# A roll of an 8192 x 8192 matrix, copied from HBM to HBM: 16 long DMAs that step by 64 rows, or 128 DMAs of 64 neighbouring rows

## The chip, the cores and the metric

One core of a Trainium2 chip. The metric is the time of one execution in microseconds on the device; where several executions are timed, their median is quoted. All ratios below are the mean time of one kernel's fast runs over the mean of the kernel before's fast runs of the same rounds, on the same chip, so they are not quite the ratio of the medians beside them.

## The reference

```python
def setup_inputs():
    return {"x": np.random.randn(8192, 8192).astype(np.float32), "shift": 100}

def reference(x, shift):
    return np.roll(x, shift, axis=1)
```

A row is 32 KiB. Each row moves right by 100 floats (400 B), and its last 100 floats come round to the front. No arithmetic is done; 268 MB have to be read and 268 MB written.

## The kernel before

With `s = 100`, `a = 128` (the shift rounded up to 512 B) and `g = 28`, the bulk of each row, 8,064 floats, is copied by DMA straight from `x` to `out`, from two issuing engines in turn (SP and ACT). In the DRAM view `j e c w`, `e` is outermost inside a DMA, so DMA engine `e` gets rows `64 c + 4 e + j` for one `j` and 32 values of `c`: its successive packets are 64 rows, or 2 MiB, apart.

```python
    engines = [nc.sync, nc.scalar]
    # ... cut
    xm = x.rearrange("(c e j) w -> j e c w", e=16, j=4)
    om = out.rearrange("(c e j) w -> j e c w", e=16, j=4)
    depth = n_rows // 64 // 4
    for c in range(4):
        for j in range(4):
            if a < n_cols:
                cs = slice(c * depth, (c + 1) * depth)
                engines[j % 2].dma_start(out=om[j, :, cs, a:], in_=xm[j, :, cs, g:n_cols - s])
```

The first 128 columns of the output go through SBUF: GpSimd issues the loads and stores, VectorE puts the pieces together. The change doesn't touch this part.

```python
    for k in range(n_st):                       # 2 steps of 4096 rows
        # ... tiles t and h cut
        for q in range(1, Q):
            nc.gpsimd.dma_start(out=t[:, q - 1], in_=lead)      # 3 loads, 512 B runs
        nc.gpsimd.dma_start(out=h[:, Q - 1, :, :s], in_=xt[k, Q - 1, :, :, n_cols - s:])
        nc.vector.tensor_copy(h[:, :Q - 1, :, :s], t[:, :, :, :s])
        if g > 0:
            nc.gpsimd.dma_start(out=h[:, 0, :, s:], in_=xt[k, 0, :, :, :g])
            nc.vector.tensor_copy(h[:, 1:, :, s:], t[:, :, :, s:])
        tiles.append(h)
    for k, h in enumerate(tiles):
        for q in range(Q):
            nc.gpsimd.dma_start(out=ot[k, q, :, :, :a], in_=h[:, q])
```

## Time and profile before

| | kernel before |
|---|---|
| median of 3 runs (first session) | 828.8 us (828.28 to 829.5) |
| span of the profiled execution | 815.4 us |
| row packets, each 32,256 B | 8,192, 4,096 a queue |

The profiled execution was 1.4% shorter than the timed ones.

The lines that carry the bound are in the prediction.

### The profile page before, as it was taken

How to read it: one execution, taken by the hardware profiler on the slowest of the kernel's cores; microseconds unless marked ns; L12 is line 12 of the kernel's file. 1: busy time of each engine (PE TensorE's matmuls, PEld its weight loads, DVE VectorE, ACT ScalarE, POOL GpSimd, SP SyncE). 2: the span in 40 equal slices, each digit the busy share in tenths (PEclk: the TensorE clock that was granted, in tenths of full speed). 3: DMA queues.
4: the chain of work that ended last, by engine and by line, in shares of the span. 5: the costliest groups of instructions: out<-in, count | busy, mean ns of one | idle time of the engine just before them, and what ended most of it. 6: DMA issues, size and time to landing. Idle time of an engine off the chain costs nothing. (4 is left out here: it accounts for less than half of the span.)

```text
span 815.4 us, 93 instructions
## 1 busy us (share of the span) xinstructions
DVE 3.7 (0%) x4; POOL 16.1 (2%) x22
## 2 busy tenths in 40 slices
DVE  0000000000000000000000000000000000000000
POOL 3000001000010000000000000000000000000000
DMA  9999999999999999999999999999999999999996
GB/s 310 341 328 347 330 349 335 337 340 346 338 337 346 338 348 348 347 333 345 340 344 337 349 326 335 334 329 334 335 329 331 329 335 334 332 331 332 329 334 250
DMA packets 10784, 272.63 MB, mean 334 GB/s; under 512 B 544, under 2 KB 544, under 8 KB 2592
## 3 DMA queue, kind: packets, MB, share of 16 engines
q10 hardware_dynamic: 4224, 132.12, 47.0%
q1 hardware_dynamic: 4224, 132.12, 46.9%
q0 software_dynamic: 2336, 8.39, 4.5%
HBM read 268.44 MB, written 268.44 MB: 658 GB/s over the span
## 5 line engine op out<-in xcount | busy, mean ns | idle before, releaser
L76 POOL DMA_DIRECT2D out_dram<-h x8 | 6.9, 954 | 170.1 <-DMA h<-in_x_dram 144.1
L67 POOL DMA_DIRECT2D t<-in_x_dram x6 | 5.4, 910 | 0.8 <-PEq L107 0.8
L69 DVE COPY h<-t 128x2400 f32<-128x2400 f32 x2 | 2.8, 1410 | 208.5 <-DMA t<-in_x_dram 208.5
L71 POOL DMA_DIRECT2D h<-in_x_dram x2 | 1.8, 883 | 28.6 <-DMA t<-in_x_dram 28.6
L68 POOL DMA_DIRECT2D h<-in_x_dram x2 | 1.8, 882 | 27.0 <-DMA t<-in_x_dram 27.0
L72 DVE COPY h<-t 128x672 f32<-128x672 f32 x2 | 1.0, 503 | 0.0
L93 POOL MEMSET const-float32-0.0<- 128x1 f32 x1 | 0.1, 99 | 0.2 <-issue 0.2
L93 POOL MEMSET const-bfloat16-1.0<- 128x1 bf16 x1 | 0.1, 103 | 0.0
L93 POOL MEMSET const-float32-1.0<- 128x1 f32 x1 | 0.1, 99 | 0.0
L93 POOL MEMSET const-uint8-127<- 128x1 uint8 x1 | 0.1, 99 | 0.0
## 6 DMA issues: line engine op xcount, KB each, us to landing
out_dram<-in_x_dram SPq DMA_DIRECT2D x8, 16128.0 KB, 401.3
out_dram<-in_x_dram ACTq DMA_DIRECT2D x8, 16128.0 KB, 400.5
out_dram<-h POOLq DMA_DIRECT2D x8, 512.0 KB, 182.5
t<-in_x_dram POOLq DMA_DIRECT2D x6, 512.0 KB, 118.2
h<-in_x_dram POOLq DMA_DIRECT2D x2, 400.0 KB, 151.3
h<-in_x_dram POOLq DMA_DIRECT2D x2, 112.0 KB, 146.1
```

The source lines that it names most:

```text
L67: nc.gpsimd.dma_start(out=t[:, q - 1], in_=lead)
L68: nc.gpsimd.dma_start(out=h[:, Q - 1, :, :s], in_=xt[k, Q - 1, :, :, n_cols - s:])
L69: nc.vector.tensor_copy(h[:, :Q - 1, :, :s], t[:, :, :, :s])
L71: nc.gpsimd.dma_start(out=h[:, 0, :, s:], in_=xt[k, 0, :, :, :g])
L72: nc.vector.tensor_copy(h[:, 1:, :, s:], t[:, :, :, s:])
L76: nc.gpsimd.dma_start(out=ot[k, q, :, :, :a], in_=h[:, q])
L93: nc = _bacc.Bacc("TRN2", target_bir_lowering=False, num_devices=1)
```

## The change

The intent: each block of 64 neighbouring rows becomes one DMA, with four neighbouring rows for each of the 16 DMA engines. Each engine gets the same rows in all, but in sequence, and there are 128 DMAs in place of 16.

```diff
-    xm = x.rearrange("(c e j) w -> j e c w", e=16, j=4)
-    om = out.rearrange("(c e j) w -> j e c w", e=16, j=4)
-    depth = n_rows // 64 // 4
-    for c in range(4):
-        for j in range(4):
-            if a < n_cols:
-                cs = slice(c * depth, (c + 1) * depth)
-                engines[j % 2].dma_start(out=om[j, :, cs, a:], in_=xm[j, :, cs, g:n_cols - s])
+    for c in range(n_rows // 64):
+        r = slice(64 * c, 64 * (c + 1))
+        if a < n_cols:
+            engines[c % 2].dma_start(out=out[r, a:], in_=x[r, g:n_cols - s])
```

## The prediction

> **What bounds the kernel now.** I read the engine table and the strip of 40 slices first, to see whether any compute engine matters at all.
>
> ```profile
> DVE 3.7 (0%) x4; POOL 16.1 (2%) x22
> DMA  9999999999999999999999999999999999999996
> GB/s 310 341 328 347 330 349 335 337 340 346 338 337 346 338 348 348 347 333 345 340 344 337 349 326 335 334 329 334 335 329 331 329 335 334 332 331 332 329 334 250
> DMA packets 10784, 272.63 MB, mean 334 GB/s; under 512 B 544, under 2 KB 544, under 8 KB 2592
> ```
>
> VectorE and GpSimd together work for 20 us out of 815. The DMA strip is at 9 or more in 39 slices and the rate is flat between 326 and 349 GB/s from the second slice on; only the last slice falls, to 250. So this is a copy that runs at one rate from start to end, and the question is what sets that rate. Next the queues and the issues.
>
> ```profile
> q10 hardware_dynamic: 4224, 132.12, 47.0%
> q1 hardware_dynamic: 4224, 132.12, 46.9%
> q0 software_dynamic: 2336, 8.39, 4.5%
> HBM read 268.44 MB, written 268.44 MB: 658 GB/s over the span
> out_dram<-in_x_dram SPq DMA_DIRECT2D x8, 16128.0 KB, 401.3
> out_dram<-in_x_dram ACTq DMA_DIRECT2D x8, 16128.0 KB, 400.5
> ```
>
> The three queues keep the 16 DMA engines busy for 98.4% of the span (47.0 + 46.9 + 4.5). Each hardware queue has 4,224 packets: 4,096 rows of 32,256 B and 8 DMAs x 16 engines = 128 completion writes. One row packet therefore takes about 0.47 x 16 x 815.4 / 4,096 = 1.50 us. "Always busy" could mean that each engine is at its own limit, or that all of them wait on a shared one. The trace's packet records (my tabulation) separate the two: the shortest row packets take 1.19 us and some 23% of them lie within 50 ns of that; the median is 1.47 us and the 90th percentile 1.83 us. An engine with nothing in its way needs 1.19 us, so 512 rows each would be 512 x 1.19 = 611 us. The other quarter of the row time is waiting for something shared.
>
> Then a table of stretches, chosen so that the GpSimd packets (which the packet records show between about 8 and 464 us of the span) are in the second and not in the third, and engines finish in the fourth and fifth.
>
> ```profile
> 20.00:120.00 100.00, 1.83 (x2) 1.77 (x2) 1.00 1.00 337
> 120.00:440.00 320.00, 1.83 (x2) 6.93 (x8) 1.00 1.00 342
> 480.00:740.00 260.00, 0.00 (x0) 0.00 (x0) 1.00 1.00 332
> 760.00:795.00 35.00, 0.00 (x0) 0.00 (x0) 1.00 0.94 335
> 795.00:815.00 20.00, 0.00 (x0) 0.00 (x0) 1.00 0.63 255
> ```
>
> The last two columns are the DMA share and GB/s. Between 760 and 795 us only 94% of the engines' time is busy, and the rate is no lower (335 against 332): when one engine stops, the others take its share. That is a shared ceiling. And it is one of HBM: a row copy loads HBM twice (read and write), a GpSimd packet once. GpSimd moves 8.39 MB in about 456 us, 18.4 GB/s. Up to 440 us: 2 x (342 - 18.4) + 18.4 = 666 GB/s of HBM traffic; after 480 us: 2 x 332 = 664. The payload rate changes by 3%, the HBM rate by 0.3%. So the kernel's time is 536.9 MB over about 665 GB/s = 807 us, and some 8 us of start and tail. Last, who waits for whom:
>
> ```profile
> SPq L37 <- DMA out_dram<-in_x_dram: 47.6, 4, 16.7
> ```
>
> Only four waits stand before an issue: a queue has four DMAs in flight, its fifth waits for the first to land.
>
> **What the Trainium skill says.** "HBM Reference", section Specifications (TRN2), gives about 716 GB/s for a pair's stack; 665 is 93% of it, so the trace agrees with a ceiling there and leaves at most 7% to win even with perfect HBM behaviour. "DMA: Bandwidth & Descriptors", section Why a DMA increments its semaphore by 16 and not by 1, says that the slowest dimension is divided over the largest k up to 16 that fits: 16 x 32 rows before and 64 rows after both give 16 engines, and the 128 completion writes per queue agree. The same page, section Latency and other measured facts, reports copies losing rate at row pitches of large powers of two: 207 GB/s at 512 KiB, 164 at 2 MiB. The kernel before steps by exactly 64 rows x 32 KiB = 2 MiB from packet to packet of a queue, which is why this change is worth doubting; yet it moves 332 GB/s each way, so its trace does not show that loss. The same page, section Issuing engines are not separate DMA queues, says that DMAs of SP and ACT interleave on the same 16 engines; the nearly equal shares of q1 and q10 agree.
>
> **The change, part by part.** Bytes, row packets (8,192 of 32,256 B) and the rows of each engine (four of every 64) stay. GpSimd's and VectorE's instructions stay, in the same order. What changes:
>
> Issues: 16 DMAs become 128, 64 a queue. The cheapest issue in the trace took 0.61 us on SP and 0.67 on ACT. 64 x 0.65 = 42 us of a sequencer that has 815: hidden.
>
> Completion writes: 256 become 2,048, so 112 more on each engine. The packet records give 9 ns each, and the other queue's next row starts about 10 ns after one. 112 x 9 ns = 1.0 us of an engine's time. As HBM, not the engine, is the ceiling, I count 0 to 1 us, say 0.5.
>
> Depth: still four DMAs in flight a queue (the built program waits on the same four semaphores in turn), but each now has 4 rows per engine for 32. A block of 64 rows takes about 812 / 128 = 6.3 us, a queue gets through one in 12.7 us, and four cover 51 us. When the oldest lands, three others (38 us of work) are queued, against an estimated 2 to 3 us for seeing it and issuing the next. No engine at the common pace runs dry. The median from issue to landing should fall from 401 to about 45 to 51 us.
>
> Skew: no engine may now be more than four blocks (about 51 us) ahead of the slowest. The completion writes show 15 engines within about 10 us of each other, and one that gains after 410 us: 17 us ahead at 501, 27 at 590, 40 at 678, done at 758 us of the span with the others at 797 to 815. The new limit would hold that one a little near the end; by the fourth row of the table above, what it doesn't use the others take. Worth 0 to -2 us in the tail.
>
> Order of rows: an engine's successive packets alternate between two neighbouring blocks 2 MiB apart and then step by 32 KiB, where before they alternated between neighbouring rows 32 KiB apart and then stepped by 2 MiB. At any moment the 16 engines still read and write rows at 128 KiB from each other, which is the larger pattern that HBM sees. I see nothing in the trace that lets me price this term: I set 0, with a spread of about 2%.
>
> Sum: 828.8 + 0.5 - 1 + 0 = about 828 us.
>
> **The rivals.** First, that the 2 MiB step cost HBM efficiency and short steps give it back. For: the skill's pitch measurement. Against: 93% of the stack's figure already. If the ceiling rose by 3% to 685 GB/s, the time would be about 828.8 - 807 x 0.029 = 805 us; I hold more than that to be very unlikely. Second, that it goes the other way: both queues now stand on the same row of two blocks at exactly 2 MiB, and all engines are held within a narrow band of blocks, so addresses that differ only in high bits collide more often. For: the same measurement. Against: HBM traffic stayed at 664 to 666 GB/s whether the engines were 2.5 us apart (first landings) or 10 and more (later), and whichever of the four rows was in turn, so the ceiling seems blind to such patterns. With 3% less it would be 854 us. Third, that the short queue starves: a fast engine waits, or issue latency shows after each landing. If each round of four blocks (16 a queue) lost 2 us it would be +32 us, 861 us; but three blocks are queued behind the oldest, so I give it little. Fourth, that the time is that of the HBM traffic and nothing moves: the base case.
>
> **Range and chances.** The base case gives 826 to 830. The order term has no price from the trace, so the range takes about 1.5% below and 2% above: 815 to 846. Faster by over 2% (below 812) needs more than 678 GB/s: 0.10. Slower by over 2% (above 845) needs a loss in HBM order or starving: 0.13. Within 2%: 0.77.
>
> **What would show it right or wrong.** Right: 5,120 packets on each hardware queue (4,096 + 1,024); DMA strip still 9 throughout; 664 to 668 GB/s of HBM traffic in the steady stretches; median landing near 50 us; about 60 waits before issues on SP, of about 12 us each, with no engine idle behind them. The starving rival would show a DMA share of 0.95 or less in the middle with row packets nearer 1.19 us. The order rivals would show a share of 1.00 with the rate, and the mean of a row packet (1.49 us), changed together. What would make me wrong is an effect of address order on HBM that neither skew nor row index brought out in the kernel before.

## More of the kernel before

```profile
out_dram<-h POOLq DMA_DIRECT2D x8, 512.0 KB, 182.5
t<-in_x_dram POOLq DMA_DIRECT2D x6, 512.0 KB, 118.2
```

A GpSimd DMA is 32 times smaller than one of SP's (512 against 16,128 KB) and still takes 118 to 182 us.

## The result, and the profile after

In the first comparison the changed kernel took 830.78 us (830.12 to 832.05, 6 runs) against 828.66 us (828.28 to 829.5, 6 runs): ratio 1.0026, 95% interval 1.0013 to 1.0039. Two repeats on other chips gave 0.9996 (0.9974 to 1.0017) and 1.0024 (1.0009 to 1.0040). So it is the same within 2%, and probably 0.2% slower.

The page after, first the DMA strip and the queues (packets, MB, share of the engines' time):

```profile
DMA  9999999999999999999999999999999999999996
q10 hardware_dynamic: 5120, 132.12, 48.6%
q1 hardware_dynamic: 5120, 132.12, 45.4%
q0 software_dynamic: 2336, 8.39, 4.7%
out_dram<-in_x_dram SPq DMA_DIRECT2D x64, 2016.0 KB, 51.1
out_dram<-h POOLq DMA_DIRECT2D x8, 512.0 KB, 154.3
t<-in_x_dram POOLq DMA_DIRECT2D x6, 512.0 KB, 102.9
```

Each hardware queue has 4,096 rows and 64 x 16 = 1,024 completion writes (one for each engine at the end of a DMA). A row DMA now lands after 51.1 us (401.3 before), and the strip is still 9 throughout. What the prediction did not name is in the last two lines: GpSimd's DMAs land 13 and 15% sooner (15 and 18% in the two controls, on one chip). Next the waits of SP's own queue (us in total, times, longest):

```profile
SPq L33 <- DMA out_dram<-in_x_dram: 748.3, 60, 15.4
```

SP waits 60 times, 12.5 us each, before it issues: the price of a short queue, paid by a sequencer that has nothing else to do. (Before, the sequencer was no freer: there a single issue of a long DMA held it for 84 us in the median, after for 0.5 us.) Last the stretches of the same windows as in the prediction (last two columns: DMA share, GB/s), of the first profile after:

```profile
20.00:120.00 100.00, 1.83 (x2) 4.39 (x5) 1.00 1.00 329
120.00:440.00 320.00, 1.83 (x2) 4.33 (x5) 1.00 1.00 337
480.00:740.00 260.00, 0.00 (x0) 0.00 (x0) 1.00 1.00 329
760.00:795.00 35.00, 0.00 (x0) 0.00 (x0) 1.00 1.00 332
```

The rates lie 1 to 2% below the first trace of before (337, 342, 332), and it is tempting to read that as the price of the new order. But that trace was of an execution of 817 us, where the timed ones took 828 us and more, and this one is of 832 us. Laid beside each other on one chip, in the controls, the two kernels have the same rates within 2 GB/s.

### The profile page after: what moved, and what is told of

It reads as the page before. It is cut to its first block, busy times and chain, and to the rows that moved or that the text cites. A ratio compares the mean times of both kernels' runs of the same rounds, so it can differ in the third digit from the quotient of the medians.

```text
span 830.2 us, 205 instructions
## 1 busy us (share of the span) xinstructions
DVE 3.7 (0%) x4; POOL 16.1 (2%) x22
## 2 busy tenths in 40 slices
DMA packets 12576, 272.64 MB, mean 328 GB/s; under 512 B 2336, under 2 KB 2336, under 8 KB 4384
## 3 DMA queue, kind: packets, MB, share of 16 engines
q10 hardware_dynamic: 5120, 132.12, 48.6%
q1 hardware_dynamic: 5120, 132.12, 45.4%
q0 software_dynamic: 2336, 8.39, 4.7%
## 6 DMA issues: line engine op xcount, KB each, us to landing
out_dram<-in_x_dram SPq DMA_DIRECT2D x64, 2016.0 KB, 51.1
```

## The experiments

Every variant replaces only the loop that copies the long part of the rows; GpSimd's part stays, and all of them gave the right result. The times in the expectations are mostly put against the first session's 828.7 us (those for two_mib_across and far_spread against 818 us), so the ratios are what to compare.

| run | rows of one DMA engine | distance between engines | DMAs | median us (kernel before) | ratio (95%) |
|---|---|---|---|---|---|
| before_again | steps of 2 MiB | 128 KiB | 16 | 819.9 (819.0) | 1.0006 (0.9982 to 1.0031) |
| after_again | 4 in sequence | 128 KiB | 128 | 818.3 (819.0) | 0.9996 (0.9974 to 1.0017) |
| after_third | 4 in sequence | 128 KiB | 128 | 820.5 (818.3) | 1.0024 (1.0009 to 1.0040) |
| short_stepped | steps of 2 MiB | 128 KiB | 128 | 824.1 (819.0) | 1.0073 (1.0049 to 1.0096) |
| long_sequence | 32 in sequence | 1 MiB | 16 | 820.7 (819.0) | 1.0026 (0.9989 to 1.0063) |
| near_engines | steps of 512 KiB | 32 KiB | 128 | 819.8 (818.0) | 1.0021 (0.9996 to 1.0045) |
| near_long | steps of 512 KiB | 32 KiB | 16 | 824.2 (819.0) | 1.0066 (1.0044 to 1.0088) |
| one_row | 1 a DMA | 32 KiB | 512 | 825.4 (818.0) | 1.0093 (1.0071 to 1.0115) |
| fourteen_engines | 5 in sequence, 14 engines | 160 KiB | 118 | 842.9 (818.0) | 1.0299 (1.0262 to 1.0337) |
| two_mib_across | 4 in sequence | 2 MiB | 128 | 1389 (818.3) | see there |
| far_engines | 4 in sequence | 16 MiB | 128 | 2157 (818.0) | see there |
| far_spread | 4 in sequence | 15.6 MiB | 128 | 827.4 (818.3) | 1.0113 (1.0084 to 1.0142) |

### The two controls

The kernels before and after, unchanged.

> The kernel before, unchanged, as a control: its first profile had a span of 815 us while its timed runs took 828.8, and the changed kernel's profile had 830. All theories: time 828.7, ratio 1.000 within 0.2%. If profiled executions of this kernel really run faster than timed ones, the span is 815 again with 664 GB/s of HBM traffic in the steady part (2 x payload); if the first profile was a lucky chip or execution, the span is 826 to 828 and the steady payload rate 328 to 330 GB/s, the same as after the change.

> The changed kernel, unchanged, as a control on the same chip as the other three. Time 830.8, ratio 1.0026 (0.1 to 0.4% above); steady payload 329 GB/s; 5,120 packets on each hardware queue.

Measured: 819.9 and 818.3 us, in profiles with spans of 818.3 and 816.5 us. Here the profiled executions are not faster than the timed ones, so the first profile of before was not typical of the session in which the 828.8 us were timed. The stretch from 480 to 740 us, before and then after (DMA share, GB/s last):

```profile
480.00:740.00 260.00, 0.00 (x0) 0.00 (x0) 1.00 1.00 332
```

```profile
480.00:740.00 260.00, 0.00 (x0) 0.00 (x0) 1.00 1.00 333
```

On this chip the same rate of 332 and 333 GB/s each way, that is 664 and 666 GB/s of HBM traffic, carries both. The change as a whole is worth nothing here in either direction.

### The two halves of the change, one at a time

short_stepped: DMAs as short as after, rows in the order of before.

```diff
+    depth = 4
+    for c in range(n_rows // 64 // depth):
         for j in range(4):
             ...   # as before
```

> Only half of the change: 128 DMAs of four rows per engine as after, but each DMA's rows step on by 64 rows as before (SP has rows 0 and 2 of each four, ACT rows 1 and 3). Theory A (the 0.26% is the price of 1,792 more completion writes, the order is free): 830 to 832, as after, with 5,120 packets a queue. Theory B (order of rows costs HBM efficiency, the size of the DMA is free): 828 to 829.5, as before. Either way GpSimd's packets should finish at about 395 us of the span rather than 464, if each completion write gives GpSimd's queue one more turn.

long_sequence: DMAs as long as before, rows in sequence.

```diff
+    for c in range(16):
+        r = slice(512 * c, 512 * (c + 1))
+        engines[c % 2].dma_start(out=out[r, a:], in_=x[r, g:n_cols - s])
```

> The other half: 16 DMAs of 32 rows per engine as before, but an engine's rows in sequence, 32 KiB from packet to packet (its 32 rows are neighbours, so engines are 1 MiB apart, where both kernels have 128 KiB). Theory A: 828 to 829.5, as before, 4,224 packets a queue. Theory B: 830 to 832, as after, or further from before, as the sequence is longer. GpSimd's packets end at about 464 us as in the kernel before. A large difference (over 2%) would mean that the distance between engines matters, which both theories leave out.

Measured: 1.0073 and 1.0026, the second with runs from 815 to 827 us and so inconclusive (it also sets the engines 1 MiB apart, so it changes more than the order). Theory A (the completion writes) wanted short_stepped to equal after, whose ratio on this chip was 0.9996; it was 0.7% above. Theory B (the order) wanted it to equal before, and failed as well. Taken by way of short_stepped, the change is two steps that cancel: short DMAs in the old order cost 0.7% (819.0 to 824.1 us), and the new order with DMAs of the same length gives 0.7% back (824.1 to 818.3 us). short_stepped was built only once, so that a build by itself makes such a difference is not excluded; three builds of after lay within 0.3% of each other. The traces say where the 0.7% is: in the stretch from 480 to 740 us short_stepped moves 329 GB/s where the controls move 332 and 333, with the same DMA share of 1.00.

```profile
480.00:740.00 260.00, 0.00 (x0) 0.00 (x0) 1.00 1.00 329
```

So the order of rows seems to move the rate by up to 1% (329 against 333 GB/s with DMAs of the same length), and not in a way that either simple theory orders. One expectation came close: GpSimd's packets ended at about 388 us of short_stepped's span (466 in the control of before), where 395 and 464 were expected.

### Is the ceiling shared, or is it the engines' own?

fourteen_engines: the same rows over 14 engines.

```diff
+    xm = x[:8190].rearrange("(c e j) w -> c e j w", e=14, j=5)
+    om = out[:8190].rearrange("(c e j) w -> c e j w", e=14, j=5)
+    for c in range(117):
+        engines[c % 2].dma_start(out=om[c, :, :, a:], in_=xm[c, :, :, g:n_cols - s])
+    nc.sync.dma_start(out=out[8190:, a:], in_=x[8190:, g:n_cols - s])
```

> Is the bound a shared ceiling or the engines themselves? Blocks of 70 rows over 14 engines instead of 64 over 16 (585 rows for each of 14, and two last rows on two engines), everything else as after. Shared HBM ceiling: 826 to 842 us, same within 2%, the mean row packet falling from about 1.50 to 1.31 us and payload staying at 328 to 335 GB/s while the engines at work are 14 (the page's DMA share then shows about 0.88). Engines bound by their own time per packet: 585 / 512 = 1.14 times as long, 930 to 950 us, packets staying at 1.49 us.

Measured 1.0299, where the shared ceiling wanted up to 2% and the engines' own limit 14%. So the run is clearly slower, and outside the range of the shared ceiling by about one per cent. From its page and its stretches:

```profile
DMA  8888888889888888888888888888888888888853
GB/s 294 345 335 332 333 341 336 342 333 344 337 336 351 336 328 342 328 344 311 340 323 337 325 334 317 331 319 336 325 333 327 319 330 327 327 313 339 322 253 132
...
480.00:740.00 260.00, 0.00 (x0) 0.00 (x0) 1.00 0.86 327
```

With 86% of the engines' time the rate is 327 GB/s, against 332 with all of it. In the packet records the mean of a row fell from 1.50 to 1.34 us (1.31 expected), and 63% of the rows took the 1.19 us that a row needs with nothing in its way (22% in the control). The ceiling is shared among the engines; that it is one of HBM is a further step, taken under one_row. The 3% are in two places: 1.5% in the steady rate, which is 12 us; and a longer tail, where the last two slices (253 and 132 GB/s, 21 us each, against about 330) cost some 18 us, where the one slow slice of before costs 5. Why the steady rate is lower and the tail longer is not shown.

### Do addresses matter at all?

far_engines: engine e has 512 rows of its own, and otherwise everything is as after. near_engines: engines on neighbouring rows.

```diff
 far_engines
+    xm = x.rearrange("(e c j) w -> c e j w", e=16, j=4)
+    om = out.rearrange("(e c j) w -> c e j w", e=16, j=4)
 near_engines
+    xm = x.rearrange("(c j e) w -> c e j w", e=16, j=4)
+    om = out.rearrange("(c j e) w -> c e j w", e=16, j=4)
 both
+    for c in range(n_rows // 64):
+        engines[c % 2].dma_start(out=om[c, :, :, a:], in_=xm[c, :, :, g:n_cols - s])
```

> Does the HBM ceiling depend on addresses at all? As after, but each engine has its own stretch of 512 rows, so that engines stand 16 MiB apart instead of 128 KiB; four rows in sequence, same DMAs and counts. Ceiling blind to order: 829 to 833 us. If far-apart high-power-of-two addresses collide[...]: 10% to 100% slower, 910 us and more, with the DMA share still 1.00 and row packets longer in proportion. In that case the agreement of before and after comes from what they share, the 128 KiB between engines.

> The opposite: as after, but the 16 engines stand on 16 neighbouring rows (32 KiB apart), and an engine steps by 16 rows (512 KiB). Ceiling blind to order: 829 to 833 us. If closeness of the 16 streams matters to HBM, over 1% either way, shown as a row packet mean away from 1.52 us at a DMA share of 1.00.

Measured: near_engines 1.0021; far_engines 2,035 to 2,233 us in four runs, 2.6 times the kernel before by the medians (its runs are too far apart for a ratio; the fastest, which was the one profiled, still took 2.5 times as long). From far_engines' page, and a stretch without GpSimd's packets:

```profile
DMA  9999999999999999999999999999999999999998
GB/s 128 125 139 129 128 135 127 129 135 137 155 132 139 152 132 145 141 144 143 126 129 132 128 144 130 130 140 138 124 133 131 134 129 143 132 128 136 133 130 117
q10 hardware_dynamic: 5120, 132.12, 48.9%
...
1000.00:1500.00 500.00, 0.00 (x0) 0.00 (x0) 1.00 1.00 132
```

The DMA strip looks like that of the kernel before, 9 in every slice, and the rate is 134 in place of 334 GB/s. A row packet takes 3.87 us in the packet records. The same bytes, packets and DMAs in the same number: only the addresses that are in flight together differ. The ceiling is far from blind to them, and the busy strip doesn't show it; only the rate does.

### Which property of the addresses?

two_mib_across: the 2 MiB step that the kernel before takes along one engine is laid across the engines. far_spread: far apart, but 500 rows instead of 512.

```diff
 two_mib_across
+    xm = x.rearrange("(c e k j) w -> c k e j w", e=16, k=16, j=4)     # om alike
+    for c in range(n_rows // 64):
+        engines[c % 2].dma_start(out=om[c // 16, c % 16, :, :, a:],
+                                 in_=xm[c // 16, c % 16, :, :, g:n_cols - s])
 far_spread
+    xm = x[:8000].rearrange("(e c j) w -> c e j w", e=16, j=4)        # om alike
+    for c in range(125):
+        engines[c % 2].dma_start(out=om[c, :, :, a:], in_=xm[c, :, :, g:n_cols - s])
+    ...   # rows 8000 to 8191 as after
```

> The kernel before steps by 2 MiB from packet to packet along one engine. Here the 2 MiB lie across the engines instead: engine e works in block e of sixteen blocks of 64 rows, four rows in sequence, all else as after. If what hurt the run with engines 16 MiB apart is that all engines share the address remainder at 2 MiB (they start each row at the same place in a 2 MiB frame), this is slow too: row packets of 2 to 4 us, 1,100 us and more. If only larger distances hurt[...], this takes 818 to 826 us.

> The engines far apart but with different remainders: engine e has 500 rows of its own (15.6 MiB from engine to engine), and 500 rows are 7 x 64 + 52, so the 16 engines have 16 different remainders at 2 MiB, as in the kernels before and after; the last 192 rows as after. If the shared remainder made the run with 16 MiB slow: back to 818 to 828 us at 330 GB/s. If distance itself did (more of HBM in use at once): again near 2,000 us.

Measured: two_mib_across 1,255 to 1,423 us, 1.7 times by the medians (again no ratio; its runs differ too much, and the profile was of one of the long ones; the fastest took 1.5 times as long). far_spread 1.0113. The steady stretch of both, in this order:

```profile
480.00:740.00 260.00, 0.00 (x0) 0.00 (x0) 1.00 1.00 207
```

```profile
480.00:740.00 260.00, 0.00 (x0) 0.00 (x0) 1.00 1.00 329
```

Engines far apart on different remainders cost about 1%; engines 2 MiB or 16 MiB apart cost a factor. Twelve rows less between engines bring the rate back from 132 to 329 GB/s. The reading I tested, that engines must not share their remainder at 2 MiB (what is left of the address after division by 2 MiB), holds for these two runs, and before, after, near_engines and far_spread all have 16 different remainders. But it isn't the whole rule: in long_sequence engines are 1 MiB apart, which gives only two remainders if they run in step, and it lost 0.3% (0.6% at most, by the interval). Did the deep queue let its engines drift apart? The traces say no. At the start of the span all engines begin their first rows together (within 0.4 us in long_sequence), and the stretch from 5 to 20 us, long_sequence first and then two_mib_across, is

```profile
5.00:20.00 15.00, 0.00 (x0) 3.44 (x4) 1.00 1.00 332
```

```profile
5.00:20.00 15.00, 0.00 (x0) 3.44 (x4) 1.00 1.00 187
```

From 20 to 105 us long_sequence moves 328 GB/s (before_again and after_again 335 and 339), and at the end of that stretch its first DMA lands on all 16 engines within 3.2 us, so they are still in step to about a row. Engines in step on two remainders thus already go at nearly the full rate, and on one remainder they do not. Where between them the loss begins, and why, is left open.

### How short may a DMA be?

one_row: blocks of 16 rows.

```diff
+    for c in range(n_rows // 16):
+        r = slice(16 * c, 16 * (c + 1))
+        engines[c % 2].dma_start(out=out[r, a:], in_=x[r, g:n_cols - s])
```

> Blocks of 16 rows, one row for each engine in a DMA: 512 DMAs, 256 a queue, with four in flight a queue as before. It quarters the queue's depth (about 12.6 us queued) and quadruples the completion writes (8,192 on the two queues). Completion theory, in proportion: after has 112 more for each engine than before and is 2.1 us longer, this has 496 more, so 828.7 + 9.4 = about 838 us. If completion writes are free under the HBM ceiling: 829 to 832. If the short queue starves the engines: over 850 us with a DMA share under 0.95 and row packets nearer 1.19 us. GpSimd's packets, with two turns a row instead of 1.25, end at about 240 to 260 us.

Measured 1.0093, or 7.4 us; the completion theory wanted 9.4, and starving over 21. From its page:

```profile
DMA  8999999999999999999999999999999999999997
out_dram<-in_x_dram SPq DMA_DIRECT2D x256, 504.0 KB, 12.7
out_dram<-h POOLq DMA_DIRECT2D x8, 512.0 KB, 97.0
t<-in_x_dram POOLq DMA_DIRECT2D x6, 512.0 KB, 66.4
```

Four DMAs of 0.5 MB in flight a queue still keep the engines busy; they land after 12.7 us. GpSimd's DMAs now land in 53 to 56% of the time of the control of before, and its packets end at 254 us (240 to 260 expected). The packet records fit one rule: from GpSimd's first packet to its last, the hardware queues moved 4,699 packets in before_again, 4,693 in after_again and 4,715 in one_row, for 2,336 of GpSimd in each. It is two hardware packets for one of GpSimd in all three, and a completion write of 9 ns counts as one of the two. Of those packets 4,571, 3,759 and 2,359 were rows. The more completion writes stand between the rows, the more turns GpSimd's queue gets.

This gives a test of what the shared ceiling is. A row copy reads and writes HBM, a GpSimd packet does only one of the two. With GpSimd's packets twice as frequent, the payload should rise and the HBM traffic stay. The stretch from 120 to 240 us, in before_again and then in one_row:

```profile
120.00:240.00 120.00, 1.83 (x2) 3.46 (x4) 1.00 1.00 337
```

```profile
120.00:240.00 120.00, 0.09 (x1) 3.47 (x4) 1.00 1.00 347
```

GpSimd's share of this is 17.7 and 35.2 GB/s in the packet records, so the HBM traffic is 2 x (337 - 17.7) + 17.7 = 656 and 2 x (347 - 35.2) + 35.2 = 659 GB/s: the payload differs by 3%, the HBM traffic by 0.5%. In one_row it is 659 from 480 to 740 us too, at a payload of 330. That speaks for HBM, or the way to it, as the ceiling. It does not hold from the start: from 20 to 120 us the same sum gives 654 in before_again and 638 in one_row.

### A version that beats both?

near_long: neighbouring rows for the engines, in 16 long DMAs.

```diff
+    xm = x.rearrange("(c e) w -> e c w", e=16)                        # om alike
+    for c in range(16):
+        cs = slice(32 * c, 32 * (c + 1))
+        engines[c % 2].dma_start(out=om[:, cs, a:], in_=xm[:, cs, g:n_cols - s])
```

> Could a version beat both, and do short DMAs cost their 0.2% in any order? The 16 engines on neighbouring rows, as in the run with neighbouring rows and short DMAs (which stood at 1.0021, 0.9996 to 1.0045), but as 16 long DMAs of 32 rows per engine, 4,224 packets a queue. If short DMAs cost 0.2% whatever the order: 0.998 to 1.001. If order sets it: 1.002 again. Under 0.995 would be a version that beats both; I do not expect it, as the HBM rate is the same 664 GB/s.

Measured 1.0066: no gain, and outside both expectations. The completion theory, which short_stepped had already failed, falls as the only cause of the small differences: this kernel has no more completion writes than before and loses 0.7%, while near_engines, with 1,792 more, loses 0.2%.

## Why the prediction was right, and where not

Sums and readings. Three are off, none of them far enough to move the forecast. 512 x 1.19 us is 609 us, not 611. The waiting in a row packet is a fifth of it (1.49 less 1.19 us), not a quarter. And "the HBM rate by 0.3%" comes from two of three stretches: the first, 337 GB/s from 20 to 120 us, gives 656 GB/s, so the HBM rate changes by 1.5% where the payload changes by 3%. one_row is the better evidence.

Time and range. Predicted 828 us on a chip where before took 828.8; measured 830.8, and the ratio lay within 0.3% of 1 in all three sessions. The step that carries it is that the time is HBM traffic over a shared rate. fourteen_engines tested the sharing with engines taken away, one_row the HBM with more of GpSimd's packets, and the controls show the same 332 and 333 GB/s on both sides. The sign of 664 to 668 GB/s of HBM traffic was missed by the first trace of after (658) and met on the later chips (666 in after_again, 664 in after_third).

Issues and depth. 60 waits of 12.5 us (predicted 60 of about 12), a median landing of 51.1 us (predicted 45 to 51), 5,120 packets a queue: as worked out. The 2 to 3 us for seeing a landing and issuing the next, for which the prediction names no source, are borne out by the trace of after: the next issue begins 0.3 to 2.8 us after the landing that it waits for, and takes 0.5 us. The starving rival falls: even a quarter of the depth keeps the strip at 9.

Completion writes. The prediction gave them 0 to 1 us, hidden under HBM. The change came out at +0.26%, -0.04% and +0.24%. one_row's 0.9% by itself would fit a cost of about 15 ns a write and engine (7.4 us over 496 more of them), but short_stepped and near_long do not fit any cost per write: short_stepped has the writes of after and took 5.8 us longer. What makes up the 0.2% stays open.

Skew. The prediction gave 0 to -2 us for holding the runaway engine back. It was gone: in the packet records the last completion writes of the engines, on both queues, lie within 12 to 13 us of each other after and 53 to 59 us before, more closely than the four-block bound of 51 us required. That the short queue did it is not shown: long_sequence and near_long, with queues as deep as before, have no runaway engine either (16 to 17 us within a queue, against 51 to 57 before). The time gained nothing from it, as a shared ceiling lets the others use what one engine leaves.

Order of rows. For the whole change the size, 0, held, but partly by luck: short_stepped says that on that chip an order term of about -0.7% met a cost of the same size for the short DMAs, which the prediction had at 0.5 us. A reason given for the 0 was wrong. The second rival was set aside because the rate stayed put with skew and row index, "so the ceiling seems blind to such patterns". far_engines shows that the ceiling loses 60% to a pattern. Skew and row index in the kernel before never take its 16 engines off their 16 different remainders, so their constancy said nothing on what happens outside. The other argument of the prediction, that the engines' 128 KiB distance is the larger pattern and is left alone by the change, fits the runs better: laying the same 2 MiB across the engines instead of along one of them costs a factor of 1.7.

What was missing. That GpSimd's part would end sooner, at about 388 us of the span in place of 466 on the same chip. It lies off the path that sets the end here; in a kernel that waits for those loads it would count.

## What to carry to other kernels

When a copy keeps all DMA engines busy, look at the rate beside the busy strip: both were 9 throughout at 334 and at 134 GB/s. Ask of a new order first which addresses the 16 engines touch at the same moment, and only then how one engine steps from packet to packet; 2 MiB and 16 MiB from engine to engine cost a factor here, while 32 KiB, 128 KiB and 1 MiB cost about 1% or less, and 500 rows in place of 512 in the split undid the loss. And where small loads share the engines with long copies, shorter copies give the small ones more turns.

## What the Trainium skill lacked or had wrong

- "DMA: Bandwidth & Descriptors", section Latency and other measured facts (HBM row pitch at large powers of two): it gives the pitch from row to row only. Here 2 MiB along one engine, in the kernel before, cost nothing that shows (332 GB/s), while 2 MiB from engine to engine gave 1,255 to 1,423 us in place of 818, and 16 MiB gave 132 GB/s. Which of the two a pitch means should be said. Its remedy, a pitch off the power of two, is borne out in kind, for the distance between engines: 500 rows in place of 512 gave 329 GB/s.
- The same page, section Queues, rings and completion order (arbitration): it says that an engine goes round its queues by packets. That a completion write takes a whole turn isn't there; here it made two hardware packets for each of GpSimd's, completion writes included (4,699, 4,693 and 4,715 for 2,336).
- "HBM Reference", section Specifications (TRN2): it has no figure for copies from HBM to HBM. (The row on pitch has one, 214 GB/s per direction called full, for rows of 16 KiB; packets of 32,256 B moved 332 here.) Here a single core's copy ran at 664 GB/s of reads and writes together, and 14 of the 16 engines still reached 654.
- No page says how far chips or sessions differ: the same kernel took 828.7 us in the first session and 818 to 819 us in four others, each on another chip. Which of the two made the difference is not shown.
